# One fp32 transformer block on one core: which products are issued in twos, matmuls of ones at the start, and parameters loaded in two pieces

## The chip, the cores and the metric

The kernel runs on one core of one Trainium2 chip. The metric is the device time of one execution in microseconds (us), as the median of several runs. A core has TensorE (PE, with its weight load shown apart as PEld), VectorE (DVE), ScalarE (ACT), GpSimd (POOL) and SyncE (SP), and 16 DMA engines. In this kernel SP issues nearly all loads.

## What is computed

One block of a model on 256 tokens with 2048 features, all in fp32, with these parts in order:

```python
h = h + 0.5 * swiglu(rmsnorm(h, ffn1_norm), ffn1_w_in, ffn1_w_out)
h = h + hybrid_mixer(rmsnorm(h, mix_norm), ...)   # short conv + chunked SSD, w_in and w_out
h = h + 0.5 * swiglu(rmsnorm(h, ffn2_norm), ffn2_w_in, ffn2_w_out)
gate = sigmoid(rmsnorm(h, ple_norm) @ ple_w_gate)
h = h + gate * (p @ ple_w_proj)
return rmsnorm(h, final_norm)
```

`swiglu(x, w_in, w_out)` is `(silu(g) * u) @ w_out` with `g, u` the halves of `x @ w_in` (inner width 5632). The mixer projects to 11296 columns, runs a causal convolution and a state-space recurrence over two chunks of 128 tokens with 32 heads, and projects back.

## The kernel before

Activations lie with features on the 128 partitions and the 256 tokens along the free axis, so `h` is 16 tiles of 128 x 256. Every weight matrix is read once, in chunks of four 128-row blocks by 256 columns (`KC = 4`, 512 KB).

**High and low parts.** To keep fp32 precision with one-pass matmuls, `parts` (line 92) loads a weight chunk `w` from SP, ACT casts it to `hi` (line 99, type fp32r), and DVE forms `lo = w - hi` (line 100). Activations are split in the same way by `split` (lines 161 and 162) into a tile whose first 256 columns are the high part and whose last 256 are the low part. Tiles come from pools: four raw buffers `w`, three each of `hi` and `lo`, two PSUM accumulators `acc`.

**A chunk.** `Gemm.chunk` (from line 114) does one chunk: for each of the two 128-column halves `j` and each of the four row blocks `k`, one **H** product (`hi` weights against the full 512 columns, high and low) and one **L** product (`lo` weights against the 256 high columns). An H and an L together are called a pair here. All go through line 135. The order of the eight products of a half is a string: by default `HLHLHLHL`. In the half `j = 0` of a full chunk whose first row block is a multiple of 16 it is `HHLLHHLL`, and in the half `j = 0` of the chunk that begins at block 8 of 16 it is `HHLLHLHL`:

```python
                order = "HL" * (k1 - k0)
                if j == 0 and k1 - k0 == KC:
                    order = {0: "HHLLHHLL", 8: "HHLLHLHL"}.get(k0 % 16, order)
```

A stretch `HHLL` is called a block, `HHLLHHLL` a double block, a single `HHLL` among pairs a lone block. A product of 16 row blocks is four chunks, 32 pairs.

**Stages.** `ffn` (from line 232) runs in three thirds of 15, 15 and 14 columns of the inner width: that many products with `w_in` (16 row blocks each), then eight products with `w_out` of 15, 15 or 14 row blocks (three full chunks and one of three or two blocks). It is called twice. The mixer has 12 products, one half-wide product for dt, 24 products between which the small SSD matmuls run, and 8 products with which norms of four groups overlap, each of 16 row blocks; then 8 products of 32 row blocks with its output matrix. The last stage has products of 16 row blocks with the gate matrix, each followed or preceded by two-block products `pr`. Norms put a few small fp32 matmuls between (`nps`, line 193, `npb`, line 220).

**The start.** The first two `w_in` products run interleaved while x is still being loaded (lines 277 to 288), in pieces of 2, 2, 4, 4 and 4 row blocks: SP loads a piece of x (line 278) and the two weight chunks, ACT and DVE split them. The norm weights and all other small parameters come in one load `sm` of 280 columns on ACT's queue (line 72), dt's parameters in another (line 74). POOL makes the constants `ident`, `ones`, `tri`, `stri`.

The order of instructions on each engine is fixed when the program is built, by a tile scheduler with priorities; each engine runs its list in order.

Of the kernel before, what the change touches and what calls it, by code (L numbers as in the profile page):

```python
# [8 lines left out]
F32 = mybir.dt.float32  # L9
F32R = mybir.dt.float32r  # L10
AF = mybir.ActivationFunctionType
# [3 lines left out]
P = 128  # L15
T = 256
D = 2048
KD = D // P
# [7 lines left out]
KC = 4  # L26
# [23 lines left out]
def block_kernel(ctx, tc, xT, pT, small, dtp, w1, o1, wm, wdt, om, w2, o2, wg, wp, out):  # L50
    nc = tc.nc
    cst = ctx.enter_context(tc.tile_pool(name="cst", bufs=1))
# [8 lines left out]
    V, A, G = nc.vector, nc.scalar, nc.gpsimd  # L61

    def aux(name):
        return aux_p.tile([P, 512], F32, tag="aux", name=name)


    warm = cst.tile([P, 1], F32, name="warm")
    V.memset(warm, 0.0)
    A.activation(out=warm, in_=warm, func=AF.Exp)
    h = cst.tile([P, KD, T], F32, name="h")  # L70
    sm = cst.tile([P, S_ALL], F32, name="sm")
    nc.scalar.dma_start(out=sm, in_=small)
    dtv = cst.tile([HEADS, 2], F32, name="dtv")
    nc.scalar.dma_start(out=dtv, in_=dtp)
    ident = cst.tile([P, P], F32, name="ident")
    make_identity(nc, ident)
    ones = cst.tile([P, P], F32, name="ones")
    G.memset(ones, 1.0)
    tri = cst.tile([P, P], F32, name="tri")
    G.affine_select(out=tri, in_=ones, pattern=[[1, P]], compare_op=ALU.is_ge, fill=0.0,  # L80
                    base=0, channel_multiplier=-1)
# [11 lines left out]
    def parts(src, nk, cols):  # L93
        w = raw.tile([P, KC, 256], F32, tag="w", name="w")
        nc.sync.dma_start(out=w[:, :nk, :cols], in_=src)
        hi = wsp.tile([P, KC, 256], F32R, tag="hi", name="hi")
        lo = wsp.tile([P, KC, 256], F32R, tag="lo", name="lo")
        with tc.high_priority(44):
            A.copy(out=hi[:, :nk, :cols], in_=w[:, :nk, :cols])  # L99
            V.tensor_tensor(out=lo[:, :nk, :cols], in0=w[:, :nk, :cols],  # L100
                            in1=hi[:, :nk, :cols].bitcast(F32), op=ALU.subtract)
        return hi, lo

    class Gemm:
# [2 lines left out]

        def __init__(self, src, K, rhs, cols=256, one=False, acc=None):  # L110
            self.src, self.K, self.rhs, self.cols, self.one = src, K, rhs, cols, one
            self.acc = acc_p.tile([P, 2, 512], F32, tag="acc", name="acc") if acc is None else acc

        def chunk(self, k0, k1):
            hi, lo = parts(self.src[:, k0:k1, :], k1 - k0, self.cols)
            for j in range(self.cols // P):
                js = slice(j * P, (j + 1) * P)
                order = "HL" * (k1 - k0)
                if j == 0 and k1 - k0 == KC:
                    order = {0: "HHLLHHLL", 8: "HHLLHLHL"}.get(k0 % 16, order)  # L120
                todo, acc, nh, nl = [], self.acc[:, j, :], k0, k0
                for part in order:
                    if part == "H":
                        k, w, nh = nh, hi, nh + 1
                    else:
                        k, w, nl = nl, lo, nl + 1
                    x, a = self.rhs(k), w[:, k - k0, js]
                    if self.one:
                        todo += [(acc[:, 0:T], a, x[:, i:i + T]) for i in ((0, T) if part == "H" else (0,))]
                    elif part == "H":  # L130
                        todo.append((acc, a, x))
                    else:
                        todo.append((acc[:, T:], a, x[:, 0:T]))
                for n, (o, a, b) in enumerate(todo):
                    nc.tensor.matmul(o, lhsT=a, rhs=b, start=(k0 == 0 and n == 0),  # L135
                                     stop=(k1 == self.K and n == len(todo) - 1))
# [6 lines left out]
    def gemm(*args, **kw):  # L143
        return Gemm(*args, **kw).all()

    def gather(acc, n=2, scale=1.0):

        lo = ev.tile([P, 2, T], F32, tag="elo", name="elo")
        A.mul(out=lo[:, :n, :], in_=acc[:, :n, T:], mul=scale)  # L149
        s = ev.tile([P, 2, T], F32, tag="esum", name="esum")  # L150
        V.scalar_tensor_tensor(out=s[:, :n, :], in0=acc[:, :n, 0:T], scalar=scale,  # L151
                               in1=lo[:, :n, :], op0=ALU.mult, op1=ALU.add)
        return s

    def split(dst, src, w=None):

        if w is None:
            A.copy(out=dst[:, 0:T], in_=src)
            V.tensor_tensor(out=dst[:, T:], in0=src, in1=dst[:, 0:T].bitcast(F32), op=ALU.subtract)
        else:  # L160
            A.activation(out=dst[:, 0:T], in_=src, func=AF.Copy, scale=w)
            V.scalar_tensor_tensor(out=dst[:, T:], in0=src, scalar=w,  # L162
                                   in1=dst[:, 0:T].bitcast(F32), op0=ALU.mult, op1=ALU.subtract)

    def new_x():
        a = blk.tile([P, 8, 512], F32R, tag="blk", name="xa")
        b = blk.tile([P, 8, 512], F32R, tag="blk", name="xb")
        return lambda k: (a if k < 8 else b)[:, k % 8, :]

    def bc2(r):  # L170
        return r.unsqueeze(1).to_broadcast([P, 2, T])
# [58 lines left out]
    def next_x(src, m, x, wcol, norm):  # L230

        norm.add(src)
        if x is not None:
            for i in range(2):
                split(x(m + i), src[:, i, :], sm[:, wcol + m + i:wcol + m + i + 1])


    def ffn(wi, wo, x, norm, wcol_next, begun=()):
        xn, nn, r = None, Norm(D, "rn"), None
        f0 = 0  # L240
        for third, nf in enumerate((15, 15, 14)):
            ga = blk.tile([P, 8, 512], F32R, tag="blk", name="ga")
            gb = blk.tile([P, 8, 512], F32R, tag="blk", name="gb")
            gx = lambda k: (ga if k < 8 else gb)[:, k % 8, :]
            held = []
            for f in range(nf):
                acc = begun[f].acc if f0 + f < len(begun) else gemm(wi[f0 + f], KD, x)
                held.append((f, gather(acc)))
                if r is None and f == 0:
                    if not begun:  # L250
                        norm.sums()
                    continue
                if r is None:
                    r = norm.spread()
                for i, s in held:
                    V.tensor_tensor(out=s, in0=s, in1=bc2(r), op=ALU.mult)
                    sg = ev.tile([P, T], F32, tag="t1", bufs=5, name="sg")
                    A.activation(out=sg, in_=s[:, 0, :], func=AF.Silu)
                    V.tensor_tensor(out=sg, in0=sg, in1=s[:, 1, :], op=ALU.mult)
                    split(gx(i), sg)  # L260
                held = []
            if third == 2:
                xn = new_x()
            for m in range(0, KD, 2):
                acc = gemm(wo[m // 2][:, f0:f0 + nf, :], nf, gx)
                s = gather(acc, scale=0.5)
                hm = h[:, m:m + 2, :]
                V.tensor_tensor(out=hm, in0=s, in1=hm, op=ALU.add)
                if third == 2:
                    next_x(hm, m, xn, wcol_next, nn)  # L270
            f0 += nf
        return xn, nn
# [2 lines left out]
    n1 = Norm(D, "rn")  # L275
    first = [Gemm(w1[f], KD, x1) for f in range(2)]
    for k0, k1 in ((0, 2), (2, 4), (4, 8), (8, 12), (12, 16)):
        nc.sync.dma_start(out=h[:, k0:k1, :], in_=xT[:, k0:k1, :])
        for k in range(k0, k1):
            split(x1(k), h[:, k, :], sm[:, S_N1 + k:S_N1 + k + 1])  # L280
        for g in first:
            if g is first[1] and k1 == KD:
                for m in range(0, KD, 2):
                    n1.add(h[:, m:m + 2, :])
                n1.sums()
            g.chunk(k0, k1)
    xm, nm = ffn(w1, o1, x1, n1, S_NM, first)

    XT = blk.tile([P, KD, T], F32, tag="blk", name="XT")
# [23 lines left out]
    for i in range(0, 24, 2):  # L313
# [9 lines left out]
        for i, s in held:  # L323
            V.tensor_tensor(out=s, in0=s, in1=bc2(rm), op=ALU.mult)
            for j in range(2):
                kind, q, _ = MIX_ORDER[i + j]
# [165 lines left out]
    for g in range(GROUPS):  # L492
        ng = Norm(512, "rg")
        for a in range(2):
            j = 4 * g + 2 * a
# [26 lines left out]


    xp, np_ = ffn(w2, o2, x2, n2, S_NP)


    nf, rp = Norm(D, "rn"), None
# [7 lines left out]
    for m in range(0, KD, 2):  # L535
        tail = m == KD - 2
        proj = lambda: gemm(wp[m // 2], 2, lambda k: px[:, k, :], one=True,
                            acc=aux("pr").rearrange("p (j t) -> p j t", j=2))
        pr = proj() if tail else None
        for q in range(2 if tail else 1):  # L540
            n = 1 if tail else 2
            acc = gemm(wg[m // 2][:, :, q * P:(q + n) * P], KD, xp, cols=n * P, one=tail)
# [98 lines left out]
```

## Time and profile before

| | |
|---|---|
| median of 3 runs | 2328.55 us (2328.32 to 2328.68) |
| the profiled execution | 2327.06 us |
| its span, first to last instruction | 2325.3 us |
| TensorE (PE) busy | 2307.8 us (99%), 13340 matmuls |
| TensorE weight load (PEld) | 2003.8 us (86%) |
| VectorE (DVE) | 1507.0 us (65%) |
| ScalarE (ACT) | 1133.6 us (49%) |
| GpSimd (POOL) | 11.8 us (1%) |
| read from HBM | 425.08 MB, 184 GB/s over the span |
| granted TensorE clock, mean | 0.998 |

Matmuls are pipelined: each is shown from its start to a modelled end, so shown durations overlap. What a matmul costs in a dense stream is the distance from its start to the start of the next. A row with "x2" stands for two of one kind in sequence, and gives the start of the first.

### The profile page before, as it was taken

Reading aid. Unit: us, or ns where it says so; the run is one execution under the profiler, and the core shown is the slowest. Engines: PE = TensorE matmul, PEld = TensorE weight load, DVE = VectorE, ACT = ScalarE, POOL = GpSimd, SP = SyncE. Lnnn points to the kernel's source line nnn. Section 1 sums busy time; section 2 is a strip of 40 time slices with the busy share of each in tenths; the row PEclk is TensorE's granted clock in tenths of the full one; section 3 lists DMA queues with packets and bytes.
Section 4 is the critical chain, followed back from the end, with each engine's and each line's share of the span. In section 5 each row is a group of like instructions: output and inputs, shape, how many; then the busy total and the mean of one; then the engine's idle time right before and its main releaser. Section 6 shows DMA issues by size and latency. Waiting matters only on the chain.

```text
span 2325.3 us, 33620 instructions
## 1 busy us (share of the span) xinstructions
PE 2307.8 (99%) x13340; PEld 2003.8 (86%) x13340; DVE 1507.0 (65%) x1928; ACT 1133.6 (49%) x1491; POOL 11.8 (1%) x25
## 2 busy tenths in 40 slices
PE   9999999999999999999999999999999999999997
PEld 7888888888888888888888888888888888888887
DVE  7665566656667777777777655566556665666776
ACT  6444444444455555444455444444444444444553
POOL 0000000000000000000000000000000000000000
PEclk9999999999999999999999999999999999999999
DMA  7666666666666565555555666666666666666654
GB/s 241 188 187 188 192 186 189 186 192 187 188 181 196 184 186 185 155 164 167 171 169 181 186 186 188 187 186 189 186 191 187 188 189 186 190 189 180 193 183 140
DMA packets 126862, 429.38 MB, mean 185 GB/s; under 512 B 13616, under 2 KB 20016, under 8 KB 126704
## 3 DMA queue, kind: packets, MB, share of 16 engines
q1 hardware_dynamic: 126144, 426.17, 60.6%
q8 instruction: 104, 1.70, 0.3%
q10 hardware_dynamic: 480, 0.80, 0.1%
q14 instruction: 54, 0.44, 0.1%
q0 software_dynamic: 80, 0.26, 0.0%
HBM read 425.08 MB, written 2.10 MB: 184 GB/s over the span
## 4 chain that ended last, share of the span: by engine, by line
PE 99%; DVE 0%; DMA 0%; ACT 0%; POOL 0%; issue 0%; DVEq 0%; POOLq 0%
PE acc L135 97%; PE pr L135 0%; PE yp L417 0%; PE yp L420 0%; PE ab L396 0%; PE npb L220 0%; DVE h L574 0%; PE xt L372 0%; PE st L385 0%; PE nps L193 0%; DMA sm<-in_small 0%; PE cb L365 0%; DVE xa L162 0%; POOL nrt L212 0%; PE dtT L432 0%; PE cs L441 0%
## 5 line engine op out<-in xcount | busy, mean ns | idle before, releaser
L100 DVE TENSOR_TENSOR lo<-w,hi 128x1024 fp32r<-128x1024 f32 (+1 forms) x834 | 990.7, 1188 | 717.5 <-ACT hi L99 710.9
L99 ACT CAST hi<-w 128x1024 fp32r<-128x1024 f32 (+1 forms) x834 | 850.8, 1020 | 1033.5 <-PE acc L135 848.6
L135 PE MATMUL acc<-xb,hi 128*128 128x512 f32 (+1 forms) x2264 | 788.5, 396 | 0.0
L135 PE MATMUL acc<-xa,hi 128*128 128x512 f32 (+1 forms) x2264 | 774.0, 395 | 5.7 <-DVE xa L162 5.7
L135 PE MATMUL acc<-xb,lo 128*128 128x256 f32 x2248 | 609.7, 282 | 0.0
L135 PE MATMUL acc<-xa,lo 128*128 128x256 f32 x2248 | 580.2, 278 | 0.0
L135 PEld LDWEIGHTS acc<-xb,hi 128*128 128x128 f32 x2264 | 413.6, 188 | 88.4
L135 PEld LDWEIGHTS acc<-xa,hi 128*128 128x128 f32 x2264 | 405.5, 188 | 80.8 <-ACT hi L99 5.7
L135 PEld LDWEIGHTS acc<-xa,lo 128*128 128x128 f32 x2248 | 422.7, 188 | 25.4 <-DVE lo L100 1.0
L135 PEld LDWEIGHTS acc<-xb,lo 128*128 128x128 f32 x2248 | 424.2, 189 | 15.3 <-issue 2.9
L135 PE MATMUL acc<-ga,hi 128*128 128x512 f32 x768 | 264.3, 396 | 0.0
L135 PE MATMUL acc<-gb,hi 128*128 128x512 f32 x640 | 222.8, 396 | 0.0
L135 PE MATMUL acc<-ga,lo 128*128 128x256 f32 x768 | 198.4, 279 | 0.0
L135 PE MATMUL acc<-gb,lo 128*128 128x256 f32 x640 | 170.6, 279 | 0.0
L135 PEld LDWEIGHTS acc<-ga,hi 128*128 128x128 f32 x768 | 137.3, 188 | 26.1
L135 PEld LDWEIGHTS acc<-ga,lo 128*128 128x128 f32 x768 | 144.6, 188 | 8.6
L135 PEld LDWEIGHTS acc<-gb,hi 128*128 128x128 f32 x640 | 116.6, 188 | 24.5
L151 DVE SCALAR_TENSOR_TENSOR esum<-acc,elo 128x512 f32<-128x512 f32 (+1 forms) x196 | 133.5, 681 | 0.0
L135 PEld LDWEIGHTS acc<-gb,lo 128*128 128x128 f32 x640 | 120.6, 188 | 4.3
L149 ACT ACTIVATE elo<-acc 128x512 f32<-128x512 f32 (+1 forms) x196 | 116.2, 593 | 0.0
L135 PE MATMUL acc<-ya,hi 128*128 128x512 f32 x256 | 88.4, 396 | 0.0
L135 PE MATMUL acc<-yb,hi 128*128 128x512 f32 x256 | 88.4, 396 | 0.0
(142 smaller groups left out, 1118.3 us busy)
## 6 DMA issues: line engine op xcount, KB each, us to landing
w<-in_w SPq DMA_DIRECT2D x350, 512.0 KB, 4.4
w<-in_wm SPq DMA_DIRECT2D x176, 512.0 KB, 4.2
w<-in_o SPq DMA_DIRECT2D x144, 512.0 KB, 3.6
w<-in_om SPq DMA_DIRECT2D x64, 512.0 KB, 3.6
w<-in_wg SPq DMA_DIRECT2D x28, 512.0 KB, 4.5
w<-in_o SPq DMA_DIRECT2D x32, 384.0 KB, 3.5
w<-in_o SPq DMA_DIRECT2D x16, 256.0 KB, 3.3
w<-in_wp SPq DMA_DIRECT2D x8, 256.0 KB, 2.6
```

The source lines that it names most:

```text
L99: A.copy(out=hi[:, :nk, :cols], in_=w[:, :nk, :cols])
L100: V.tensor_tensor(out=lo[:, :nk, :cols], in0=w[:, :nk, :cols], in1=hi[:, :nk, :cols].bitcast(F32), op=ALU.subtract)
L135: nc.tensor.matmul(o, lhsT=a, rhs=b, start=(k0 == 0 and n == 0), stop=(k1 == self.K and n == len(todo) - 1))
L149: A.mul(out=lo[:, :n, :], in_=acc[:, :n, T:], mul=scale)
L151: V.scalar_tensor_tensor(out=s[:, :n, :], in0=acc[:, :n, 0:T], scalar=scale, in1=lo[:, :n, :], op0=ALU.mult, op1=ALU.add)
```

## The change

Three edits. In `Gemm.chunk` the half `j = 0` at row block 0 of 16 keeps its double block; the lone block in the half `j = 0` at row block 8 is gone (`HLHLHLHL` there now); and products made with `twice=True`, the default, have a second double block in the half `j = 1` of the chunk at row block 8. The products in `ffn` are made with `twice=False`. At the start, `ones` is now written by DVE, and eight fp32 matmuls of `ones` with itself (128 x 128, into a PSUM tile that nobody reads) stand first in PE's list. The first 16 columns of the small parameters, which hold the first norm's weights, are loaded alone on ACT's queue, followed there by the second tile of x; the first tile of x is loaded alone on SP's queue; the other 264 columns and dt's parameters follow on SP's queue behind the last piece of x. The table load for Exp comes behind the two loads on ACT.

```diff
--- before.py
+++ after.py
@@ -66,16 +66,21 @@
 
     warm = cst.tile([P, 1], F32, name="warm")
     V.memset(warm, 0.0)
-    A.activation(out=warm, in_=warm, func=AF.Exp)
     h = cst.tile([P, KD, T], F32, name="h")
     sm = cst.tile([P, S_ALL], F32, name="sm")
-    nc.scalar.dma_start(out=sm, in_=small)
+    nc.scalar.dma_start(out=sm[:, 0:KD], in_=small[:, 0:KD])
+    nc.sync.dma_start(out=h[:, 0:1, :], in_=xT[:, 0:1, :])
+    nc.scalar.dma_start(out=h[:, 1:2, :], in_=xT[:, 1:2, :])
+    A.activation(out=warm, in_=warm, func=AF.Exp)
     dtv = cst.tile([HEADS, 2], F32, name="dtv")
-    nc.scalar.dma_start(out=dtv, in_=dtp)
+    ones = cst.tile([P, P], F32, name="ones")
+    V.memset(ones, 1.0)
+
+    idle = aux("idle")
+    for _ in range(8):
+        nc.tensor.matmul(idle[:, 0:P], lhsT=ones, rhs=ones, start=True, stop=True)
     ident = cst.tile([P, P], F32, name="ident")
     make_identity(nc, ident)
-    ones = cst.tile([P, P], F32, name="ones")
-    G.memset(ones, 1.0)
     tri = cst.tile([P, P], F32, name="tri")
     G.affine_select(out=tri, in_=ones, pattern=[[1, P]], compare_op=ALU.is_ge, fill=0.0,
                     base=0, channel_multiplier=-1)
@@ -107,8 +112,8 @@
 
 
 
-        def __init__(self, src, K, rhs, cols=256, one=False, acc=None):
-            self.src, self.K, self.rhs, self.cols, self.one = src, K, rhs, cols, one
+        def __init__(self, src, K, rhs, cols=256, one=False, acc=None, twice=True):
+            self.src, self.K, self.rhs, self.cols, self.one, self.twice = src, K, rhs, cols, one, twice
             self.acc = acc_p.tile([P, 2, 512], F32, tag="acc", name="acc") if acc is None else acc
 
         def chunk(self, k0, k1):
@@ -116,8 +121,8 @@
             for j in range(self.cols // P):
                 js = slice(j * P, (j + 1) * P)
                 order = "HL" * (k1 - k0)
-                if j == 0 and k1 - k0 == KC:
-                    order = {0: "HHLLHHLL", 8: "HHLLHLHL"}.get(k0 % 16, order)
+                if k1 - k0 == KC and (k0 % 16 + j == 0 or self.twice and k0 % 16 + j == 9):
+                    order = "HHLLHHLL"
                 todo, acc, nh, nl = [], self.acc[:, j, :], k0, k0
                 for part in order:
                     if part == "H":
@@ -244,7 +249,7 @@
             gx = lambda k: (ga if k < 8 else gb)[:, k % 8, :]
             held = []
             for f in range(nf):
-                acc = begun[f].acc if f0 + f < len(begun) else gemm(wi[f0 + f], KD, x)
+                acc = begun[f].acc if f0 + f < len(begun) else gemm(wi[f0 + f], KD, x, twice=False)
                 held.append((f, gather(acc)))
                 if r is None and f == 0:
                     if not begun:
@@ -262,7 +267,7 @@
             if third == 2:
                 xn = new_x()
             for m in range(0, KD, 2):
-                acc = gemm(wo[m // 2][:, f0:f0 + nf, :], nf, gx)
+                acc = gemm(wo[m // 2][:, f0:f0 + nf, :], nf, gx, twice=False)
                 s = gather(acc, scale=0.5)
                 hm = h[:, m:m + 2, :]
                 V.tensor_tensor(out=hm, in0=s, in1=hm, op=ALU.add)
@@ -275,7 +280,11 @@
     n1 = Norm(D, "rn")
     first = [Gemm(w1[f], KD, x1) for f in range(2)]
     for k0, k1 in ((0, 2), (2, 4), (4, 8), (8, 12), (12, 16)):
-        nc.sync.dma_start(out=h[:, k0:k1, :], in_=xT[:, k0:k1, :])
+        if k0 > 0:
+            nc.sync.dma_start(out=h[:, k0:k1, :], in_=xT[:, k0:k1, :])
+        if k0 == 12:
+            nc.sync.dma_start(out=sm[:, KD:], in_=small[:, KD:])
+            nc.sync.dma_start(out=dtv, in_=dtp)
         for k in range(k0, k1):
             split(x1(k), h[:, k, :], sm[:, S_N1 + k:S_N1 + k + 1])
         for g in first:
```

PE's list in the first `ffn`, third product with `w_in`, its head and then the start of row block 8 (`xa` and `xb` are the two halves of the split activations), before:

```order
L135 MATMUL acc<-xa,hi 128x512 x2
L135 MATMUL acc<-xa,lo 128x256 x2
L135 MATMUL acc<-xa,hi 128x512 x2
L135 MATMUL acc<-xa,lo 128x256 x2
L135 MATMUL acc<-xa,hi 128x512
L135 MATMUL acc<-xa,lo 128x256
...
L135 MATMUL acc<-xb,hi 128x512 x2
L135 MATMUL acc<-xb,lo 128x256 x2
L135 MATMUL acc<-xb,hi 128x512
L135 MATMUL acc<-xb,lo 128x256
```

The double block heads the product, and a lone block stands at row block 8. PE's list at the same two places, of the change:

```order
L140 MATMUL acc<-xa,hi 128x512 x2
L140 MATMUL acc<-xa,lo 128x256 x2
L140 MATMUL acc<-xa,hi 128x512 x2
L140 MATMUL acc<-xa,lo 128x256 x2
L140 MATMUL acc<-xa,hi 128x512
L140 MATMUL acc<-xa,lo 128x256
...
L140 MATMUL acc<-xb,hi 128x512
L140 MATMUL acc<-xb,lo 128x256
```

The lone block is gone: from the double block at the head of the product to the next product's double block there are now 28 pairs in a row.

PE's list in the mixer's fifth product, from the last pair of row block 7 on, before:

```order
L135 MATMUL acc<-xa,hi 128x512
L135 MATMUL acc<-xa,lo 128x256
L135 MATMUL acc<-xb,hi 128x512 x2
L135 MATMUL acc<-xb,lo 128x256 x2
L135 MATMUL acc<-xb,hi 128x512
L135 MATMUL acc<-xb,lo 128x256
```

It has the same lone block as a `w_in` product. PE's list in the same product, from the last pair of the half `j = 0` of the chunk at row block 8 on, of the change:

```order
L140 MATMUL acc<-xb,hi 128x512
L140 MATMUL acc<-xb,lo 128x256
L140 MATMUL acc<-xb,hi 128x512 x2
L140 MATMUL acc<-xb,lo 128x256 x2
L140 MATMUL acc<-xb,hi 128x512 x2
L140 MATMUL acc<-xb,lo 128x256 x2
L140 MATMUL acc<-xb,hi 128x512
```

A second double block stands there, 16 pairs behind the first and 8 pairs ahead of the next product.

ACT's list at the start of the program, before (`an` is made of dt's parameters):

```order
L72 DMA sm<-in_small 128x280
L69 ACT_TABLE_LOAD
L69 ACTIVATE warm<-warm 128x1
L74 DMA dtv<-in_dtp 32x2
L161 ACTIVATE xa<-h,sm 128x256 x2
L99 CAST hi<-w 128x512
L181 ACTIVATE sq<-h 128x512
L99 CAST hi<-w 128x512
L341 ACTIVATE an<-dtv 32x1
```

The load of all small parameters and the table load come first. ACT's list at the same place, of the change:

```order
L71 DMA sm<-in_small 128x16
L73 DMA h<-in_xT 128x256
L74 ACT_TABLE_LOAD
L74 ACTIVATE warm<-warm 128x1
L166 ACTIVATE xa<-h,sm 128x256 x2
L104 CAST hi<-w 128x512
L186 ACTIVATE sq<-h 128x512
L104 CAST hi<-w 128x512
```

Two loads now stand ahead of the table load, and `an` has left this stretch.

## Rows read from the trace of the kernel before

**Rows 1.** The page: busy us of each engine (share of the span), instructions.

```profile
PE 2307.8 (99%) x13340; PEld 2003.8 (86%) x13340; DVE 1507.0 (65%) x1928; ACT 1133.6 (49%) x1491; POOL 11.8 (1%) x25
```

**Rows 2.** Timeline of PE, `w_in` products of the first ffn: start us, us, engine, operation.

```profile
36.94 0.63 PE L135 MATMUL acc<-xb,hi 128*128 128x512 f32 x2
...
37.63 0.40 PE L135 MATMUL acc<-xb,hi 128*128 128x512 f32 x1
...
37.98 0.40 PE L135 MATMUL acc<-xb,hi 128*128 128x512 f32 x1
...
38.35 0.40 PE L135 MATMUL acc<-xb,hi 128*128 128x512 f32 x1
...
42.59 0.62 PE L135 MATMUL acc<-xa,hi 128*128 128x512 f32 x2
...
43.98 0.40 PE L135 MATMUL acc<-xa,hi 128*128 128x512 f32 x1
...
48.14 0.63 PE L135 MATMUL acc<-xb,hi 128*128 128x512 f32 x2
...
53.79 0.62 PE L135 MATMUL acc<-xa,hi 128*128 128x512 f32 x2
```

**Rows 3.** The same view, `w_out` products of 15 row blocks.

```profile
187.47 0.63 PE L135 MATMUL acc<-ga,hi 128*128 128x512 f32 x2
...
188.87 0.40 PE L135 MATMUL acc<-ga,hi 128*128 128x512 f32 x1
...
193.11 0.63 PE L135 MATMUL acc<-gb,hi 128*128 128x512 f32 x2
...
193.81 0.40 PE L135 MATMUL acc<-gb,hi 128*128 128x512 f32 x1
...
197.97 0.62 PE L135 MATMUL acc<-ga,hi 128*128 128x512 f32 x2
...
199.36 0.39 PE L135 MATMUL acc<-ga,hi 128*128 128x512 f32 x1
...
203.52 0.62 PE L135 MATMUL acc<-gb,hi 128*128 128x512 f32 x2
```

**Rows 4.** The same view, a `w_out` product of 14 row blocks.

```profile
679.40 0.64 PE L135 MATMUL acc<-ga,hi 128*128 128x512 f32 x2
...
680.81 0.40 PE L135 MATMUL acc<-ga,hi 128*128 128x512 f32 x1
```

**Rows 5.** The same view, a gate product behind the `pr` products.

```profile
2235.19 0.63 PE L135 MATMUL acc<-xa,hi 128*128 128x512 f32 x2
...
2236.58 0.40 PE L135 MATMUL acc<-xa,hi 128*128 128x512 f32 x1
...
2240.82 0.63 PE L135 MATMUL acc<-xb,hi 128*128 128x512 f32 x2
```

**Rows 6.** Timeline of ACT at the start (in brackets: idle before, and what ended it).

```profile
4.22 0.91 ACT L161 ACTIVATE xa<-h,sm 128x256 fp32r<-128x256 f32 x2 [1.47 <-DMA sm<-in_small]
```

**Rows 7.** Timeline of PE and its weight load at the start.

```profile
5.69 0.80 PE L135 MATMUL acc<-xa,hi 128*128 128x512 f32 x1 [5.69 <-DVE xa L162]
...
7.44 0.63 PE L135 MATMUL acc<-xa,hi 128*128 128x512 f32 x1
...
13.52 0.19 PEld L135 LDWEIGHTS acc<-xa,lo 128*128 128x128 f32 x1 [0.33 <-DVE lo L100]
```

**Rows 8.** Busy time by stretch: us, then each engine's busy us and instructions.

```profile
9.10:13.10 4.00, 4.00 (x24) 3.47 (x23) 3.97 (x10) 3.86 (x8) 0.00 (x0) 1.00 0.98 371
```

**Rows 9.** Timeline of PE: the fp32 matmuls `npb` (two records each).

```profile
30.83 0.71 PE L220 MATMUL npb<-ident,nrt 128*128 128x128 f32 x4
31.30 0.71 PE L135 MATMUL acc<-xa,hi 128*128 128x512 f32 x2
```

**Rows 10.** The same view: the longest stretch of pairs behind a lone block.

```profile
22.56 0.40 PE L135 MATMUL acc<-xb,hi 128*128 128x512 f32 x1
...
28.11 0.40 PE L135 MATMUL acc<-xb,hi 128*128 128x512 f32 x1
```

## The prediction

> **What bounds the kernel now.** I read the page first: PE is busy 2307.8 us, 99% of the span, DVE 65%, ACT 49% [rows 1]. So apart from the first microseconds every gain or loss is in the distance from one matmul's start to the next. I then read PE's timeline, start by start, in the first `w_in` products. The reader is to see two rhythms in it. From 37.63 to 42.59 us there are 14 pairs in 4.96 us, 0.3543 us each; from 43.98 to 48.14 there are 12 pairs in 4.16 us, 0.3467 each [rows 2]. Operands, shapes and clock are the same. I call them slow and fast. In the slow one the spacing repeats every three pairs (0.35, then 0.37: [rows 2], 37.63 to 38.35), in the fast one every two.
>
> What sets the rhythm is the block that was passed last. A lone block at 36.94 turns fast to slow; the double block at 42.59 turns slow to fast; the next lone block at 48.14 ends that [rows 2]. So each `w_in` product now has 12 fast pairs and 14 slow ones, and takes 53.79 - 42.59 = 11.20 us.
>
> **The rule of the rhythms.** The `w_out` products show that it isn't simply "a double block is good". The double block at 187.47 comes behind 12 slow pairs and leaves the stream slow: 188.87 to 193.11 is 4.24 us for 12 pairs [rows 3]. The lone block at 193.11, again behind 12 slow pairs, turns it fast (193.81 to 197.97, 4.16 us). And the double block at 197.97 is entered in the fast rhythm and leaves it fast (199.36 to 203.52, 4.16 us); it takes 1.39 us [rows 3]. I read along the whole timeline, and one rule fits every block inside a stream of pairs:
>
> - from fast, one block leads to slow, a second right behind it back to fast (31 double blocks entered fast in the products with no small matmul between: all stay fast);
> - from slow it depends on how many pairs n came since the slow rhythm began. With n a multiple of 3, one block leads to fast, so a double one ends slow again. With n of remainder 2 a double block ends fast (14 pairs, as at 42.59). With remainder 1 it ends slow (10 pairs, as at 679.40, where it takes 680.81 - 679.40 = 1.41 us [rows 4]).
>
> **The change, part by part.** *FFN `w_in`, `twice=False`.* The lone block goes, the double block stays. Entered fast, each product is 1.39 + 28 x 0.3467 = 11.10 us against 11.20: 0.10 less. After the norm's small matmuls the first double block leaves fast today, and the norm's own part of the list does not change. Of 88 products I count 85: -8.5 us.
>
> *FFN `w_out`.* Today 187.47 to 197.97 is 10.50 us. With 26 fast pairs: 1.39 + 26 x 0.3467 = 10.40, 0.10 less; the other product of the couple starts with 12 fast pairs, and the lone block and the slow pairs stand behind them, so the same sum holds but for roundings. I take 0.085, a little under the difference of rows that are rounded to 0.01, for all 48 (those of 14 row blocks are not worked out apart): -4.1 us.
>
> *Mixer, `twice=True`.* Behind the first double block come 16 pairs, then the second, then 8. Entered fast, all stay fast: 0.10 for each 16 row blocks. The first 12 products: -1.2. The output matrix, 8 products of two times 16, the first broken by a norm: 14 x 0.10 = -1.4. The 24 products with SSD matmuls between: these restart the rhythm in the middle of a product, so between 0 and 24 x 0.10 = 2.4; I take -1.3, the middle. The 8 products with group norms: every second one starts slow today; 16 pairs have remainder 1, so their second double block would end slow too. I take 0, with 0.5 either way.
>
> *Gate products.* This is where the change costs. The double block behind `pr` ends slow: 2236.58 to 2240.82 is 4.24 us for 12 pairs; the lone block at 2240.82 then makes it fast [rows 5]. After the change 16 slow pairs come first (remainder 1), the second double block ends slow, and 8 more slow pairs follow. Against today 12 pairs turn from fast to slow (12 x 0.0076 = 0.09) and a block takes the longer 1.41 [rows 4]: +0.1 for each of five, less 0.1 for the first, which starts fast: +0.4.
>
> *Start.* ACT waits 1.47 us for `sm` until 4.22 [rows 6]; the first 16 columns and one tile of x are much less to load, so up to 1.47 us can go, a little less since the table load now stands behind a second issue. The first real matmuls run at the lower clock, 1.2 GHz: 0.63 us shown for 512 columns at 7.44 [rows 7], 0.40 later [rows 2]. From 5.69 to 13.52 PE issues 16 pairs and an H in 7.83 us, 0.33 of it waiting for DVE [rows 7]; at 0.354 a pair these are 5.9 us, so 1.6 us is what a clock that is already high could give. But DVE is busy 3.97 of 4.00 us from 9.10 to 13.10 [rows 8], and PE waits for it at 13.52: a PE that starts earlier and faster waits there for longer. I take 0.6 us, near the low end, because DVE is full. The low end is a loss: four `npb` records take 0.47 us [rows 9], so the 16 records of the eight fp32 matmuls take 1.9 us at the upper clock and up to 3.8 at the lower; from about 1.2 us on they end by 5.0, hidden ahead of the old first matmul at 5.69, and hold back the new one by 0.3 at most. So +0.3 to -1.5 for the range. What is moved to SP's queue (264 columns of `sm`, dt's parameters) is two issues ahead of a weight chunk; their readers are `an`, which moves back in ACT's list, and stages from the first `w_out` on, and the loads are covered as long as raw buffers stay ahead of PE. Uncovered, they would cost under 1 us once.
>
> The sum: 8.5 + 4.1 + 1.2 + 1.4 + 1.3 + 0 - 0.4 + 0.6 = 16.7 us. The profiled execution took 2327.06 us (span 2325.3 and 1.8 around it), 1.5 less than the median of the runs, so 2310.4 for a like one, and 2328.55 - 16.7 = **2311.9 us** for the median.
>
> [...] The rows show 0.3467 and 0.3543 for one and the same pair [rows 2], so here the neighbours do count.
>
> **Rivals.**
> *The order gives nothing.* The rhythm could be tied to something that only goes along with the blocks, such as waits for `hi` and `lo` at a chunk's start. Against it: one and the same double block leaves fast or slow by the count of pairs alone [rows 2, 3]. Then only the start remains: 2328.55 - 0.6 = 2328.0. Chance 0.04.
>
> *The trap (slower).* A `w_in` product that starts slow has 28 slow pairs ahead of the next double block: remainder 1, which ends slow. Without the lone block nothing takes it out until the first `w_out` products, where 26 pairs have remainder 2. Such a product costs 1.40 + 28 x 0.3543 = 11.32, 0.22 above forecast and 0.12 above today. It can be entered if the state behind a norm comes out otherwise, or if the fast rhythm lapses: 28 pairs without a block are more than the trace has; the longest is 16, 22.56 to 28.11, 5.55 us, 0.3469 each, with no drift [rows 10]. A lapse would hit all six thirds: 85 x 0.22 = 18.7, and the products of 14 row blocks (24 pairs, a multiple of 3, slow again) would add 16 x 24 x 0.0076 = 2.9: 2311.9 + 21.6 = 2333.5. From five trapped thirds on the kernel is slower than before, with all six by 0.2%. Chance 0.04, of which 0.03 for the lapse.
>
> *A part of the thirds is trapped.* One to three of six, 3.1 to 9.4 us, or the mixer gains nothing: 2315 to 2322. Chance 0.08. For it: the state behind a norm depends on when its small matmuls end. Against: both FFNs leave that point fast today.
>
> **How the numbers follow.** The forecast has the remaining 0.84. Its own bounds: SSD products 1.3 either way, start +0.9 and -0.9, norm and gate products 0.5 each way: 2309 to 2315. The range goes on to one trapped third, 2317.5, and down to 2308.5 for bounds that add up. A measurement of this kernel tells 0.2%, 4.7 us, from no change. Faster by more than that are the forecast and most of the partial case: 0.91; within 0.2%, the case of no effect and the remainders of the two trapped cases: 0.06; slower by over 0.2%, the lapse: 0.03.
>
> **What would show it.** Right: PE's timeline in `w_in` has double blocks 11.10 us apart and 0.347 a pair throughout; `w_out` products of 10.40 us; the gate products slow from end to end; the first real matmul before 5 us, shown 0.40 long, with a longer wait for DVE behind it. Wrong: stretches of 28 pairs in 9.92 us (trap), or pairs of 0.354 in places where no block or small matmul came before.

## The result, and the profile after

The changed kernel took 2316.47 us in the median of four runs (2313.87, 2315.93, 2317.01, 2318.19), the kernel before 2328.44; the ratio is 0.9948 [0.993, 0.9965]. That is faster by 12.0 us, inside the range, 4.6 us above the forecast of 2311.9. Two numbers call for an explanation: the forecast isn't reached, and the runs lie 4.3 us apart where those of before lie within 0.4.

The page of the changed kernel, its span and its busy times, beside [rows 1]:

```profile
span 2312.2 us, 33652 instructions
PE 2297.4 (99%) x13356; PEld 2000.0 (86%) x13356; DVE 1507.5 (65%) x1929; ACT 1133.3 (49%) x1491; POOL 11.7 (1%) x24
```

PE still fills the span; the profiled run (2313.87) is 13.2 us shorter than that of before (2327.06). PE's timeline after, `w_in` products of the first FFN, beside [rows 2] (columns as there):

```profile
43.81 0.63 PE L140 MATMUL acc<-xa,hi 128*128 128x512 f32 x2
...
45.21 0.40 PE L140 MATMUL acc<-xa,hi 128*128 128x512 f32 x1
...
54.91 0.63 PE L140 MATMUL acc<-xa,hi 128*128 128x512 f32 x2
```

From double block to double block it is 11.10 us, and the 28 pairs from 45.21 to 54.91 take 9.70, 0.3464 each: fast to the end, with no lapse. A `w_out` product of 15 row blocks after, beside [rows 3], now takes 10.40 us:

```profile
187.42 0.62 PE L140 MATMUL acc<-ga,hi 128*128 128x512 f32 x2
...
197.82 0.63 PE L140 MATMUL acc<-ga,hi 128*128 128x512 f32 x2
```

A gate product behind `pr` after, beside [rows 5]:

```profile
2221.06 0.63 PE L140 MATMUL acc<-xa,hi 128*128 128x512 f32 x2
...
2222.45 0.40 PE L140 MATMUL acc<-xa,hi 128*128 128x512 f32 x1
...
2228.10 0.64 PE L140 MATMUL acc<-xb,hi 128*128 128x512 f32 x2
...
2232.34 0.40 PE L140 MATMUL pr<-px,hi 128*128 128x256 f32 x2
```

Sixteen pairs in 5.65 us, 0.353 each: slow, through both double blocks, 11.28 us in all. The two profiled executions by section (start of its first product matmul to start of the next section's; us):

| section | before | after | difference | forecast |
|---|---|---|---|---|
| first matmul, and the two first products | 5.69 + 25.61 | 6.26 + 26.37 | +1.3 | -0.6 |
| `w_in`, 86 products (85 in the forecast) | 964.2 | 955.8 | -8.4 | -8.5 |
| `w_out`, 48 products | 492.4 | 488.4 | -4.0 | -4.1 |
| mixer: first 12, and dt | 140.89 | 139.90 | -1.0 | -1.2 |
| mixer: 24 with SSD | 305.11 | 304.53 | -0.6 | -1.3 |
| mixer: 8 with group norms | 94.80 | 94.77 | 0 | 0 |
| mixer: output | 180.33 | 179.09 | -1.2 | -1.4 |
| gate products, with `pr` | 98.35 | 98.68 | +0.3 | +0.4 |
| last norm's `npb` | 1.16 | 2.07 | +0.9 | not counted |
| behind the last matmul | 8.79 | 8.29 | -0.5 | not counted |

These add up to -13.2, the difference of the spans. So the terms of the order are near their forecast, but for the SSD products at half of theirs; the start and the tail are not. In the view of ACT's start after, beside [rows 6], the first tile of x is split at 3.19, but the second, alone on ACT's queue, is waited for until 5.19:

```profile
3.19 0.51 ACT L166 ACTIVATE xa<-h,sm 128x256 fp32r<-128x256 f32 x1
5.19 0.51 ACT L166 ACTIVATE xa<-h,sm 128x256 fp32r<-128x256 f32 x1 [1.49 <-DMA h<-in_xT]
```

PE's timeline of the same stretch, beside [rows 7]:

```profile
1.16 3.67 PE L81 MATMUL idle<-ones 128*128 128x128 f32 x16 [1.16 <-DVE ones L77]
6.26 0.50 PE L140 MATMUL acc<-xa,hi 128*128 128x512 f32 x1 [1.44 <-ACT hi L104]
7.21 0.40 PE L140 MATMUL acc<-xa,hi 128*128 128x512 f32 x1
...
8.49 0.63 PE L140 MATMUL acc<-xa,hi 128*128 128x512 f32 x1
...
14.89 0.19 PEld L140 LDWEIGHTS acc<-xa,lo 128*128 128x128 f32 x1 [0.83 <-DVE lo L105]
```

ACT splits the second tile before it casts the first weight chunk, so `hi` comes late and the first real matmul starts at 6.26 instead of 5.69. The 5.69 is an early draw of the old start: in the four other traces with it (the order alone, the trap and the two with lone blocks, below) `sm` is there at 4.48 to 4.78 instead of 4.22, and the first matmul starts at 5.95 to 6.25, here in the first kernel with lone blocks:

```profile
6.25 0.80 PE L137 MATMUL acc<-xa,hi 128*128 128x512 f32 x1 [6.25 <-DVE xa L164]
```

The third product starts at 31.49 to 32.43 in these four, at 31.30 in the profile of before and at 32.63 in that of the change. So a part of the +1.3 in the table is the draw of one profile.

The clock is up at 7.21 (0.40 shown), behind the ones and 1.44 us without a matmul, and down again at 8.49 (0.63). The stretch around it, columns as in [rows 8], has the granted clock in the third column from the end, 0.53:

```profile
7.80:11.00 3.20, 3.20 (x12) 2.71 (x11) 3.20 (x10) 2.89 (x7) 0.00 (x0) 0.53 0.83 292
```

Later, as forecast, the wait for DVE has grown, from 0.33 to 0.83.

The time of one run therefore doesn't explain a median 2.6 us above it. Two theories went to the chip: **one**, that the clock's fall in the start or the tail comes and goes from run to run; **two**, that a third of the first FFN is entered slow in some runs and trapped there.

### The profile page after: what moved, and what is told of

Its sections match the earlier page's. It is cut to its first block, busy times and chain, and to the rows that moved or that the text cites. A ratio compares the mean times of both kernels' runs of the same rounds, so it can differ in the third digit from the quotient of the medians.

```text
span 2312.2 us, 33652 instructions
## 1 busy us (share of the span) xinstructions
PE 2297.4 (99%) x13356; PEld 2000.0 (86%) x13356; DVE 1507.5 (65%) x1929; ACT 1133.3 (49%) x1491; POOL 11.7 (1%) x24
## 4 chain that ended last, share of the span: by engine, by line
PE 99%; DVE 0%; issue 0%; DMA 0%; POOL 0%; ACT 0%; POOLq 0%; ACTq 0%; DVEq 0%
PE acc L140 97%; PE pr L140 1%; PE yp L426 0%; PE yp L429 0%; PE ab L405 0%; DMA h<-in_xT 0%; PE nps L198 0%; PE npb L225 0%; PE xt L381 0%; PE st L394 0%; POOL hw L578 0%; DVE lo L105 0%; DVE xa L167 0%; PE cb L374 0%; ACT hi L104 0%
## 5 line engine op out<-in xcount | busy, mean ns | idle before, releaser
L140 PE MATMUL acc<-gb,lo 128*128 128x256 f32 x640 | 177.3, 277 | 0.0
```

## The experiments

Where no other start is named, a kernel has the start of the kernel before; "order" is the change of `Gemm.chunk` and of `twice` alone.

**The changed kernel again.** No edit.

> The changed kernel once more, for its spread and a second trace. Theory one (the clock at the start and end): runs spread over some 4 us again, 2313.5 to 2318.5, because eight matmuls of ones raise the clock early and an idle PE behind them lets it fall again, in a place that differs from run to run; the FFN products stay at 11.10 and 10.40 us. Theory two (trapped thirds): the spread comes from thirds of an FFN that start slow in some runs; then a trace of a slower run shows w_in products of 11.3 us, 3 us more for each such third.

Measured: 2313.78 (2312.84 to 2316.83), ratio 0.9937 [0.9924, 0.9949]. The run that was profiled is the slowest of the five. PE's timeline of it, the same place as above:

```profile
32.17 0.70 PE L225 MATMUL npb<-ident,nrt 128*128 128x128 f32 x4
32.62 0.71 PE L140 MATMUL acc<-xa,hi 128*128 128x512 f32 x2
...
44.00 0.63 PE L140 MATMUL acc<-xa,hi 128*128 128x512 f32 x2
...
55.28 0.64 PE L140 MATMUL acc<-xa,hi 128*128 128x512 f32 x2
```

Here it is 11.28 us from double block to double block. The 13 products take 146.96 us against 144.39 in the run above, the first `w_out` section 83.45 against 83.25; the five other thirds agree within 0.01. That is the trap, in one third: 2.6 + 0.2 = 2.8 us, and 2316.83 - 2.8 = 2314.0. Theory two explains this run, theory one doesn't: its start shows the same fall of the clock. The fall does come and go (the granted clock from 7.5 to 11 us is 0.50 to 0.66 in three of the eight traces with the ones, 1.00 in the five others), but the third product starts at 32.52 to 32.63 with it and at 31.72 to 32.46 without, too little for 4.3 us.

**The order alone, and the start alone.** The second has the order of before:

```diff
-                if k1 - k0 == KC and (k0 % 16 + j == 0 or self.twice and k0 % 16 + j == 9):
-                    order = "HHLLHHLL"
+                if j == 0 and k1 - k0 == KC:
+                    order = {0: "HHLLHHLL", 8: "HHLLHLHL"}.get(k0 % 16, order)
```

> The order of the products as changed, with the start of before. Theory one: the order alone gives 15.5 us (FFN 12.4, mixer 1.6, its output 1.2, gate +0.3), so 2312.5 to 2313.5, with a spread under 1 us like before's, and the first real matmul at 5.7 us. Theory two: 2316 to 2317 with a spread of 3 us or more, since the trapped thirds come with the order and not with the start.

> The start as changed, with the order of before. Theory one: the start loses 1.3 us or more and spreads the runs: 2329.5 to 2333. The forecast's own value was a gain of 0.6: 2327.8. Theory two leaves the start without effect: 2328 to 2329, spread under 1 us.

Measured: the order alone 2313.85 (2313.31 to 2316.85), ratio 0.9938 [0.9925, 0.995]; the start alone 2328.61 (2328.10 to 2330.64), ratio 1.0001 [0.9992, 1.001]. The order gives all of the gain that can be seen. Of the start no gain is seen, but the interval reaches 1.9 us down, so it doesn't exclude the 0.6 of the forecast. Theory two had the spread of the order alone right, 3.5 us, and its median wrong: only one of the five runs lies at 2316 to 2317. The start alone spreads over 2.5 us where under 1 was expected; the 21 runs of the kernel before beside it spread over 2.0 (2327.62 to 2329.66).

**The trap, set on purpose.** The order, with a lone block at the head of the fourth `w_in` product of each third:

```diff
+                if self.lone and k0 + j == 0:
+                    order = "HHLLHLHL"
...
+ gemm(wi[f0 + f], KD, x, twice=False, lone=f == 3)
```

> As order_only, but the fourth w_in product of each third has a lone block at its head in place of the double block: six blocks less in the whole program. By the rule of the rhythms the lone block turns fast to slow, 30 pairs later (a multiple of 3) the double block ends slow, and 28 pairs on (remainder 1) each one after it ends slow too: 70 products at 0.21 us more, 14.7; the first w_out product behind each of the four 15s 0.18 more; all products of 14 row blocks 0.17 more, 2.7: 18 us in all over order_only, about 2331. If double blocks set the fast rhythm whatever came before, only the six products lose, 0.2 each: 1.2 us over order_only.

Measured: 2331.16, ratio 1.0007 [0.9998, 1.0016]. So one block out of place in six products gives back the whole gain of the order. PE's timeline, a product behind that block in the second third:

```profile
326.50 0.64 PE L137 MATMUL acc<-xa,hi 128*128 128x512 f32 x2
...
337.80 0.64 PE L137 MATMUL acc<-xa,hi 128*128 128x512 f32 x2
```

It stays at 11.30 us to the end of the third. The ten runs form two groups, three at 2327.8 to 2328.6 and seven at 2331.1 to 2332.1. The profiled one is of the lower group, and its first third is fast:

```profile
31.49 0.71 PE L137 MATMUL acc<-xa,hi 128*128 128x512 f32 x2
...
42.86 0.64 PE L137 MATMUL acc<-xa,hi 128*128 128x512 f32 x2
...
53.97 0.63 PE L137 MATMUL acc<-xa,hi 128*128 128x512 f32 x2
...
65.07 0.62 PE L137 MATMUL acc<-xa,hi 128*128 128x512 f32 x2
...
76.17 0.63 PE L137 MATMUL acc<-xa,hi 128*128 128x512 f32 x2
```

It had entered slow (11.37 us from 31.49 to 42.86), and the lone block at 42.86, behind 28 slow pairs, turned it fast (11.11 us to the next head). That is the rule's remainder 1 seen block by block: the first one leads to fast, so the second one of a double block leads back to slow. The two groups are 3 us apart, one third's worth, as the draw at the first norm would make them; of the upper group there is no trace.

**A second double block in `w_in` too.** The changed kernel, with

```diff
- gemm(wi[f0 + f], KD, x, twice=False)
+ gemm(wi[f0 + f], KD, x)
```

> The changed kernel with the second double block in the w_in products of the FFNs too. By the rule a product that starts slow has 16 pairs to the second double block (remainder 1, still slow) and 8 more to the next product's (remainder 2, fast): the trap of the first third opens after one product. So no runs near 2316.8 or above, spread under 2 us around 2314; the extra block costs 0.006 us in each of 88 products, 0.5 us, against untrapped runs. If the spread of the changed kernel came from the start or the clock, it stays at 3.5 to 4 us.

Measured: 2314.59 (2313.36 to 2316.38), 0.9939 [0.9925, 0.9953]. In its trace the first third entered slow; 16 slow pairs (34.02 to 39.67) and the second double block left it slow, then 8 pairs (41.06 to 43.89, remainder 2) and the next head's double block turned it fast:

```profile
34.02 0.40 PE L140 MATMUL acc<-xa,hi 128*128 128x512 f32 x1
...
39.67 0.63 PE L140 MATMUL acc<-xb,hi 128*128 128x512 f32 x2
...
41.06 0.40 PE L140 MATMUL acc<-xb,hi 128*128 128x512 f32 x1
...
43.89 0.62 PE L140 MATMUL acc<-xa,hi 128*128 128x512 f32 x2
...
55.00 0.62 PE L140 MATMUL acc<-xa,hi 128*128 128x512 f32 x2
```

The 13 products take 144.65 us instead of 146.96; the price is 0.1 us for each 15 products. The spread of 3.0 is wider than expected; the run at 2316.38 has no trace and stays unexplained.

**Lone blocks where a product starts slow.** The order, a second double block in `w_in`, and at the heads behind `pr`, behind the group norms and in the second half of the first output product a lone block in place of the double one:

```diff
+                if k0 == self.lone and j == 0:
+                    order = "HHLLHLHL"
```

> The start of before, the order as changed, two double blocks in w_in as well, and a lone block in place of the first double one where small matmuls leave the stream so that a double block ends slow: the gate products behind pr, the three products behind nps in the group norms, the second half of the first output product. By the rule these run fast: gate 5 x 0.18 = 0.9 us less, the others 0.3 to 0.5: 2312 to 2313, spread under 2 us. If the rhythm behind small matmuls is set by chance, no gain: 2314.

> lone_heads once more, with the start of before, as the reference for the three starts that run beside it: 2313.2, spread about 1 us.

Measured: 2313.15 (2312.98 to 2314.12) and, once more, 2312.43 (2312.19 to 2312.67), 0.9931 [0.9919, 0.9944]. PE's timeline of the gate product in the second run:

```profile
2221.08 0.63 PE L137 MATMUL acc<-xa,hi 128*128 128x512 f32 x2
...
2228.02 0.62 PE L137 MATMUL acc<-xb,hi 128*128 128x512 f32 x2
...
2232.18 0.40 PE L137 MATMUL pr<-px,hi 128*128 128x256 f32 x2
```

It is 11.10 us instead of 11.28. The runs lie within 1.1 and 0.5 us.

**Double blocks everywhere, and none.** The two lines of the order become `if k1 - k0 == KC: order = "HHLLHHLL"`; in the other kernel they are gone. Both have the start of the change.

> Double blocks in every half of every full chunk, so there are hardly any pairs in which a rhythm could run. A double block takes 1.393 us in either state, 0.348 a pair: some 1200 more of them cost 0.006 each against fast pairs, 7 us, and save 0.007 for each of the 400 pairs that are slow now, 2.8. So 2318 to 2319, with no trapped runs: spread under 2 us. If double blocks themselves gave the time, more of them would be faster than the changed kernel.

> No blocks at all, pairs everywhere. By the rule nothing changes the rhythm between two interruptions, and each FFN runs through in the rhythm that its norm leaves: all fast 11.094 us a w_in product, all slow 11.32. Both fast: 2313; one FFN slow: 14.5 more, 2327; both: 2342. The trace shows one rhythm in each FFN from the norm to its end. If blocks are what keeps a stream fast, both are slow in all runs and 28 or more fast pairs without a block don't last.

Measured: everywhere 2318.71, 0.9957 [0.9944, 0.997]; none 2347.98 (2345.38 to 2350.82), 1.0082 [1.0069, 1.0095]. PE's timeline of the kernel with none, first FFN:

```profile
31.45 0.70 PE L223 MATMUL npb<-ident,nrt 128*128 128x128 f32 x4
31.91 0.48 PE L138 MATMUL acc<-xa,hi 128*128 128x512 f32 x1
...
766.57 0.40 PE L138 MATMUL acc<-xb,hi 128*128 128x512 f32 x1
...
766.93 0.50 PE L196 MATMUL nps<-ones,nacc 128*128 128x1 f32 x4
```

From 31.91 to 766.93 there are 2080 pairs in a row in 735.0 us, 0.3534 each. The state the norm left is kept until the next norm. Measured is 6 us above the slower of the expected cases, 2342, which were for the FFNs: these are 26.6 us longer in the trace than in that of the change (29 expected), and the mixer, which I had not counted, is 7.6 longer.

**Three starts without the trap.** The kernel with lone blocks, with the start of the change; then without the matmuls of ones; then, with them, the first two tiles of x in one load on SP's queue:

```diff
-    idle = aux("idle")
-    for _ in range(8):
-        nc.tensor.matmul(idle[:, 0:P], lhsT=ones, rhs=ones, start=True, stop=True)
...
-    nc.sync.dma_start(out=h[:, 0:1, :], in_=xT[:, 0:1, :])
-    nc.scalar.dma_start(out=h[:, 1:2, :], in_=xT[:, 1:2, :])
+    nc.sync.dma_start(out=h[:, 0:2, :], in_=xT[:, 0:2, :])
```

> The order of lone_heads, in which no third can stay slow, with the start of the change. Theory: the second tile of x lands at 5.0 to 5.2 us on ACT's queue, so the first real matmul comes at 6.1 to 6.3 as with the old start; and the clock that the ones raise falls again. The start is worth nothing: 2313.2 to 2314.2. The forecast's value: 2312.6. If the start makes the spread of the changed kernel, this one spreads over 3 us.

> As lone_new_start, without the eight matmuls of ones. Theory: PE waits for ACT's hi, not behind the ones, and the clock rises once, at 9 to 10.5 us, not early and again at 10.9: within 0.5 us of lone_new_start. If the ones give what they are there for, it is 1 us or more slower.

> As lone_new_start, but both first tiles of x in one load on SP's queue, as before. Theory: the late second tile on ACT's queue is what takes the gain of the small parameters' early landing; on SP's queue it lands by about 4.0, the first real matmul comes at about 5.0 and is no more than the DVE chain can follow: 0.5 to 1 us less than lone_new_start. If the loads share the DMA engines so that the queue does not matter, the same as lone_new_start.

Measured, against 2312.43 with the old start: 2312.75 (2312.13 to 2313.34), 2312.5 (2311.99 to 2313.41) and 2311.77 (2311.63 to 2313.36). With the new start and no trap the spread is 1.2, so the start doesn't make the spread. In this pair of traces the ones raise the clock: the first real matmul is shown 0.49 long with them and 0.80 without.

```profile
6.21 0.49 PE L142 MATMUL acc<-xa,hi 128*128 128x512 f32 x1 [1.27 <-ACT hi L104]
```

```profile
6.04 0.80 PE L139 MATMUL acc<-xa,hi 128*128 128x512 f32 x1 [6.04 <-DVE xa L166]
```

They don't do it in every run: in three of the eight traces with the ones (the start alone, double blocks everywhere, none) the first real matmul is shown 0.79 or 0.80 long, behind idle times of 1.11 to 1.27 us, here in the start alone:

```profile
6.21 0.79 PE L140 MATMUL acc<-xa,hi 128*128 128x512 f32 x1 [1.27 <-ACT hi L104]
```

What becomes of a raised clock is in the busy times from 13.10 to 17.10 us (columns as in [rows 8]), with ones:

```profile
13.10:17.10 4.00, 3.11 (x16) 2.50 (x17) 3.75 (x6) 3.59 (x8) 0.00 (x0) 1.00 1.00 390
```

and without:

```profile
13.10:17.10 4.00, 4.00 (x25) 3.48 (x24) 3.86 (x7) 4.00 (x8) 0.00 (x0) 1.00 1.01 393
```

With ones PE is ahead, and idles for 0.89 of these 4.00 us; without them it idles for none. The third product starts 0.34 us earlier with them (32.22 against 32.56), which the medians don't show. The last of the three starts, ACT's and PE's first steps:

```profile
3.89 0.91 ACT L167 ACTIVATE xa<-h,sm 128x256 fp32r<-128x256 f32 x2 [1.14 <-DMA sm<-in_small]
...
5.36 0.50 PE L141 MATMUL acc<-xa,hi 128*128 128x512 f32 x1 [0.42 <-DVE xa L168]
```

Both tiles are split at 3.89, and the first matmul starts at 5.36 instead of 6.2. The median is 1.0 us lower than with the second tile on ACT's queue, but the ranges overlap, so I take it as likely, not as shown. It has the lowest median of all versions, ratio 0.993 [0.9918, 0.9943].

## Why the prediction was right and wrong

*Right: the rule of the rhythms and its sizes.* `w_in` was forecast at 11.10 and is 11.10, `w_out` 10.40 and 10.40, a gate product 0.1 more and 0.09. The same rule, with other blocks, gave the times of the trap and of double blocks everywhere, and the lone blocks that freed the gate products. With the same products in another order, the kernel without blocks takes 2347.98 us and the changed one 2313.78 in its second measurement, 34.2 less. The page *TensorE: Matmul & The Clock Gate* of the Trainium skill says in "Back-to-back issue gap" that in a stream weight load and matmul together set the spacing, and gives N / 2.4 + 2.5 ns for a matmul by itself; the order of a stream is no term there, and in this case it is one.

*Held by its upper end: the range.* The forecast's own bounds were 2309 to 2315. The median of 2316.47 lies in the range because that was carried on for one trapped third, a case with a chance of 0.08, and which median four runs give hangs on how many of them were trapped; the second one, 2313.78, lies within the bounds. The ends of that case are loose: 3.1 us on 2311.9 is 2315.0 and 9.4 is 2321.3, where the prediction has 2317.5 and 2322.

*Wrong: "both FFNs leave that point fast today".* I took the state behind the first norm from one profiled run, and priced the trap for whole kernels, at 0.04 and 0.08. It is drawn anew in each run: of the ten traces with the double block at this head and the change's `w_in` order (with or without the second block), the third product is slow in five (11.36 to 11.38 us to the next head) and fast in five (11.18 to 11.20). In the second FFN it is fast in all ten. The lone block of before can't keep such a draw: behind 12 slow pairs it turns fast [rows 3], so a product that is entered slow ends fast, and only one product differs. That fits its runs, which lie 0.4 us apart in the first measurement and 2.0 in 21 runs, with no second group; that block was itself the reset which I priced only as a loss. Without it a slow entry costs 0.2 us in each of 13 products. The traced run shows one trapped third; the runs at 2315.93, 2317.01 and 2318.19 have no trace. The last of them lies 1.4 us further up than one trapped third explains; what that is stays open. Of the nine runs of the changed kernel five are at 2312.8 to 2314.1, four at 2315.9 and above; the first measurement had three of these four, so its median lies in the upper group.

*Wrong: "I take 0.6 us" for the start.* No gain was seen (ratio 1.0001, and the median 0.3 us higher without the trap); the runs can't tell 0.6 from 0, but the step behind it failed: the first matmul, "before 5 us" in my list, came at 6.04 to 6.26 in the traces of this start, where the old one has 5.69 to 6.25. I had taken the old start, too, from one profile. My sum had the small `sm` and one tile of x, but not that ACT splits two tiles before its first cast: the second tile's load behind `sm` on ACT's queue landed at 5.2. And the clock, which I priced at up to 1.6 us, gives 0.3 in the one pair of traces that tells it, and PE waits for ACT and DVE in the rest: my reason for the low value held, further than I took it.

*Missized: the SSD products*, 0.6 for the middle value of 1.3, within its bounds. *Not counted: the tail.* Last to run are the `npb` of the last norm, 1.16 us before:

```profile
2315.39 1.16 PE L220 MATMUL npb<-ident,nrt 128*128 128x128 f32 x8 [1.08 <-POOL nrt L212]
```

and in the changed kernel:

```profile
2301.80 2.07 PE L225 MATMUL npb<-ident,nrt 128*128 128x128 f32 x8 [1.08 <-POOL nrt L217]
```

The granted clock is 0.96 of full speed in the first stretch and 0.50 in the second, behind the same idle times. In two profiles of the kernel with lone blocks they took 1.53 and 1.16, so this too is drawn per run, between 1.2 and 2.1.

The first profiled run came out 3.5 us above the 2310.4 that I had for a like one: 1.9 of it is that run's start against the early one of before, 0.9 the tail, 0.7 the SSD products, and the rest of the rows nearly cancel. The nine runs of the changed kernel together have a median of 2314.12, 2.2 above the forecast.

## What to carry to other kernels

In a dense stream of matmuls of two widths, read the distance from start to start: a state that costs 2% may be set by the two or three matmuls that stand first in another order, and be kept for hundreds of microseconds. Judge such an order by what it does to both states, not by its time in the state that one profile shows; a block that resets the state can be worth its price. And before a first matmul is made earlier or faster, look at what feeds the second and the tenth.

## What the runs showed that I had not expected

The rhythm has no visible end: 2080 pairs at 0.3534 us in a row, and in the same kernel's mixer 76 at the fast one, both without a block. What in the engine holds a rhythm, and what decides the draw behind the first norm, no run here shows. In the profile of the change the clock that 3.67 us of ones had raised fell again while real matmuls ran, from 0.40 shown at 7.21 to 0.63 at 8.49. And a tile of 128 KB that was issued second on ACT's queue landed at 5.2 us, while one load of two tiles, 256 KB, on SP's queue was there when ACT got `sm` at 3.89.
